# Statistics of all tokens ahead of the first projection, and one bank for both broadcasts, in a two-layer decoder trunk

## The chip, the cores and the metric

The kernel runs on one core of one Trainium2 chip, in one launch. The metric is the device time of that launch in microseconds (us). The kernel before has a median of 1230.92 us over three runs (1229.31, 1230.92 and 1232.93).

Names used throughout: PE is TensorE (matrix products, fp32 results in banks of PSUM), DVE is VectorE, ACT is ScalarE, POOL is GpSimd, SP issues the loads. A "stage" is a stretch of the program, and "k" counts the eight 128-row slices of the 1024 model features.

## The reference

There is one sequence of 512 tokens with 1024 features, two layers, and a conditioning vector c:

```python
def trunk(x, c):                         # cut to what matters
    c_act = silu(c)
    for i in range(2):
        sh1, sc1, g1, sh2, sc2, g2 = split(c_act @ w_mod[i] + b_mod[i], 6)
        h = rms_norm(x, norm_mix[i]) * (1 + sc1) + sh1
        y = stick_breaking_attention(h) if i == 0 else s5_ssm(h)
        x = x + g1 * y
        h = rms_norm(x, norm_ffn[i]) * (1 + sc2) + sh2
        x = x + g2 * conv_ffn(h)         # up-projection, conv of width 3, silu gate, down-projection
    sh, sc = split(c_act @ w_fin + b_fin, 2)
    return rms_norm(x, norm_out) * (1 + sc) + sh
```

`rms_norm` divides each token by the root of the mean square of its 1024 features. So every sub-layer begins with a statistic of each token, which all its 1024 features wait for. The attention's first product is v = h @ w_v, then k and q.

## The kernel before, in words

**Layout.** x stays on the chip, transposed: eight tiles `x[k]` of 128 features by 512 tokens. A product with fp32 accuracy is made of three fast ones (`mm3`, L140 to L146): each operand is split into a high part and a low remainder, and high by high (L142), high by low (L145) and low by high (L146) are summed in a PSUM bank. A weight tile of 128 by 1024 is loaded (`load_w`, L135), ACT writes its high part (L136), and DVE the remainder (L137).

**Normalising.** PE sums the squares over features (`stat`, L234), a matmul of one column for each 128 tokens. ACT takes the root (L238), five small DVE operations invert it (L239 to L243), DVE writes it as diagonals `dg` (L251), and PE broadcasts these over all partitions with a product by ones, which is `rbc` (L256; in the first stage L490). `norm_tile` (L270) then makes one tile of h: DVE multiplies x by rbc into `nt` (L274), ACT applies scale and shift twice (into `hH`, rounded, L284, and into fp32, L285), and DVE subtracts the two to get `hL` (L286).

**Modulation.** The vectors sh, sc and g are matrix-vector products on DVE, one of 128 by 1024 each (`gemv_step`, L167). Those of the first normalisation (16 of them, buffers `wgs`) are made in the first stage, two for each k, ahead of that k's scale and shift.

**First stage** (L471 to L523). The squares are summed on ACT and DVE while x arrives. The statistics run for tokens 0 to 255, and later, behind the first `nt`, for tokens 256 to 511. The two rbc lie in two banks. Tiles k = 0 and 1 are normalised in two halves of 256 tokens, the others whole. Eight banks hold v; each k adds 24 products of 512 columns to them, 192 in all.

**Heads.** The three other sub-layers (feed-forward 0, the state-space layer, feed-forward 1) begin alike: four output banks are filled with tokens 0 to 255 for k = 0 to 7, then with tokens 256 to 511. The statistics of the second half are computed inside the first: at k = 2 its `stat`, and at k = 6 its `rbc` (L256), into a bank of its own. The state-space head computes u, the others `up`.

**What sets the order.** A scheduler puts the instructions of each engine in an order by its own estimate of when their inputs are ready; instructions marked by `keep_in_program_order` (`pe_pin`) keep theirs, and `behind_head` lets some begin only after a given instruction. Each engine then works through its list strictly in order, and waits at an instruction until the semaphores of its inputs have been raised. PE's order in the heads is that of the code: for a k, the four products of hH by the high weights, then the pairs with the low parts.

Of the kernel before, what the change touches and what calls it, by code (L numbers as in the profile page):

```python
# [16 lines left out]
P = 128  # L17
# [50 lines left out]
for _k, _w in _COLS:  # L68
    _OFF[_k] = _n
    _n += _w  # L70
NSMALL = _n

OUT_SHAPE = (2, D * T // 2)
# [7 lines left out]
def _trunk(ctx, tc, I, out, tap):  # L81
# [15 lines left out]
    def bank(p=None, name="ps"):  # L97
        p = p or mm
        return p.tile([P, 512], F32, tag="b", name=name)
# [75 lines left out]
    def mcol(l, v, j):  # L175
        return l * 48 + v * 8 + j
# [77 lines left out]
    def rstd_bc(R, cr, pl, pinned=False):  # L254
        bc = bank(pl, "rbc")
        ins = PE.matmul(bc[:, cr], ones, R["dg"][:, cr], start=True, stop=True)  # L256
        if pinned:
            pe_pin(ins)
        R["bc"][cr.start] = bc
# [9 lines left out]

    def norm_tile(h, k, bc, a, b, cr=FULL, perm=False):  # L270
# [3 lines left out]
        pin["nt"] = V.tensor_tensor(t, x[k][:, cr], bc[:, cr], ALU.mult)  # L274
        first = cr.start == 0 and k == HEADK
        hh, hl = h[0][k][:, cr], h[1][k][:, cr]
        hf = hh.bitcast(F32)
        src = t
        if perm:
            hh, hl = half_cols(h[0][k], cr), half_cols(h[1][k], cr)  # L280
            hf = hh.bitcast(F32)
            u = u.rearrange("p (j c) -> p j c", j=CH)
            src = t.rearrange("p (c j) -> p j c", j=CH)
        act = S.activation(hh, src, AF.Identity, bias=b[:, k:k + 1], scale=a[:, k:k + 1])  # L284
        aff = S.activation(u, src, AF.Identity, bias=b[:, k:k + 1], scale=a[:, k:k + 1])  # L285
        dve = V.tensor_tensor(hl, u, hf, ALU.subtract)  # L286
        if first:
            pin["head"] = [act, aff, dve]
# [80 lines left out]
    def ffn(l, R, prep=None, last=None, hook=lambda: None):  # L369
# [4 lines left out]
        with ExitStack() as fc:  # L374
# [37 lines left out]
            for gi, gn in enumerate((8, 8, 6)):  # L412
# [4 lines left out]
                if gi == 0:  # L417
# [52 lines left out]
    def attention(acc):  # L470
        with ExitStack() as ac:  # L471
            ap = ac.enter_context(tc.tile_pool(name="attn", bufs=1, reuse_waits="tile"))
            wgs = ap.tile([P, 4, D], F32, tag="vn", name="wgs")

            def wmod(col, q):
                SP.dma_start(wgs[:, q, :], I["w_modT"][col * P:(col + 1) * P, :])

            wmod(mcol(0, 1, 0), 0)
            SP.dma_start(consts, I["consts"])
            wmod(mcol(0, 0, 0), 1)  # L480
            SP.dma_start(small, I["small"])
            wv0 = load_w(I["w_v"][0:P, :], name="wv0")
            R = rstd_new(acc)
            R["bc"] = {0: bank(aux, "rbc"), T // 2: bank(mm, "rbc")}
            rb = np_.tile([P, T], F32, tag="sq", bufs=2, name="rb")

            def stat(cr):
                R["ps"] = bank(aux if cr.start == 0 else mm, "stat")
                pin["dg", cr.start] = [rstd_stat(R, cr)]
                PE.matmul(R["bc"][cr.start][:, cr], ones, R["dg"][:, cr], start=True, stop=True)  # L490

            stat(HALF[0])
            h = new_h()
            a = cp.tile([P, KD], F32, tag="Amix0", name="Amix0")
            vb = [bank(mm if i < 6 else aux, f"v{i}") for i in range(8)]
            p0 = None
            for k in range(KD):
                with behind_head(p0) if k in (1, 2) else ExitStack():
                    for v in (1, 0):
                        with behind_head(pin["sum"] if v else pin["dg", 0]):  # L500
                            gemv_step(mcol(0, v, k), False, wgs[:, (2 * k + 1 - v) % 4, :], k > 0)
                    for v in (1, 0):
                        c = mcol(0, v, k)
                        S.activation(mod[:, c:c + 1], raw[:, c:c + 1], AF.Identity, bias=sm("b_mod", c, 1))
                wn = sm("norm_mix", k, 1)
                S.activation(a[:, k:k + 1], mod[:, mcol(0, 1, k):mcol(0, 1, k) + 1], AF.Identity, bias=wn, scale=wn)
                for cr in HALF if k < 2 else (FULL,):
                    if k == 0 and cr.start:
                        with behind_head([pin["nt"]]):
                            stat(cr)  # L510
                        for c in HALF:
                            S.activation(rb[:, c], R["bc"][c.start][:, c], AF.Copy)
                    norm_tile(h, k, R["bc"][cr.start] if k < 2 else rb, a, mod[:, 0:KD], cr)
                    if k == 0:
                        p0 = [pin["nt"]]
                w = wv0
                if k:
                    with behind_head(p0) if k in (1, 2) else ExitStack():
                        w = load_w(I["w_v"][k * P:(k + 1) * P, :], name=f"wv{k}")
                for i in (0, 1, 4, 5, 2, 3, 6, 7):  # L520
                    nb, tt = divmod(i, 4)
                    mm3(vb[i], (h[0][k][:, tt * P:(tt + 1) * P], h[1][k][:, tt * P:(tt + 1) * P]),
                        (w[0][:, nb * 512:(nb + 1) * 512], w[1][:, nb * 512:(nb + 1) * 512]), k == 0, k == KD - 1)  # L523
            last_load = pin["load"]
# [428 lines left out]
    def ssm(R):  # L953
# [3 lines left out]
        with ExitStack() as zc:  # L957
# [4 lines left out]
            for cr in HALF:  # L962
                for k in range(KD):
                    if cr.start == 0 and k == 2:
                        rstd_stat(R, HALF[1], True)
                    if cr.start == 0 and k == 6:
                        rstd_bc(R, HALF[1], mm, True)
                    norm_tile(h, k, R["bc"][cr.start], a, b, cr, perm=True)
                    for w, ps in hd:
# [180 lines left out]
    S.activation(crow, crow, AF.Silu)  # L1150
    sqrt_table()
    pc = [bank(name=f"pc{q}") for q in range(2)]
    for q in range(2):
        PE.matmul(pc[q], ones[0:1, :], crow[:, q * 512:(q + 1) * 512], start=True, stop=True)
    for k in range(KD):
        sq = acc if k == 0 else np_.tile([P, T], F32, tag=("sq", "nt1")[k % 2], bufs=2, name="sq")
        for cr in HALF if k > 6 else (FULL,):
            act = S.activation(sq[:, cr], x[k][:, cr], AF.Square)
            if k:
                add = V.tensor_tensor(acc[:, cr], acc[:, cr], sq[:, cr], ALU.add)  # L1160
                if cr.stop == T // 2:
                    pin["sum"] = [add]
    with behind_head([act]):
        for q in range(2):
            S.activation(cact[:, q * 512:(q + 1) * 512], pc[q], AF.Copy)
    R = attention(acc)
# [163 lines left out]
```

## Time and profile before

| | |
|---|---|
| median of three runs | 1230.92 us |
| the profiled execution | 1231.03 us |
| its span, first to last instruction | 1229.2 us |
| mean granted TensorE clock | 0.987 |
| v stage: first product to last | 19.39 to 69.94 us |
| rbc of the second half in the heads | 292.38 (feed-forward 0), 680.40 (state space), 865.40 us (feed-forward 1) |

A timeline row gives the start, the duration, the engine and line, the operation with its output and inputs, how many alike were joined (x4), and in brackets the idle time before it on its engine with what ended it. Matmuls of a row overlap, so the distance of starts tells the pace better than the duration. A row of windows gives, after the stretch and its length, the busy time and number of instructions on PE, PE's weight loads, DVE, ACT and POOL, then the granted PE clock, the busy share of the DMA engines, and GB/s.

### The profile page before, as it was taken

To read this page: it belongs to the slowest core of one execution; us is meant where nothing else is said; L and a number is where in the kernel's file an instruction comes from. 1 tells how busy PE (TensorE), PEld (TensorE's weight loads), DVE (VectorE), ACT (ScalarE), POOL (GpSimd) and SP (SyncE) were. 2 spreads that over 40 slices of the span, in tenths; PEclk is the share of its full clock that TensorE was granted. 3 is DMA by queue.
4 is the path that set the end of the run, shared out by engine and by line. 5 is a ranking of instruction groups with operands and counts; after the bars stand their busy time and mean duration, and the time that the engine had idled before them with its cause. 6 is when DMAs were issued, how large, how long until landed. Compare 5 with 4: busy or idle time off the path is not lost. (4 is left out here: it accounts for less than half of the span.)

```text
span 1229.2 us, 16696 instructions
## 1 busy us (share of the span) xinstructions
PE 1176.7 (96%) x6244; PEld 967.3 (79%) x6244; DVE 890.1 (72%) x1335; ACT 561.1 (46%) x870; POOL 269.8 (22%) x265
## 2 busy tenths in 40 slices
PE   6999999899999999899998989999999999999997
PEld 4777776589887888678878867689988888888887
DVE  7858888848978778786877559587688458744645
ACT  7646656447543243322345824554843234422434
POOL 1000000000896959876800001000000000000003
PEclk9999999899999999999999989999999999999999
DMA  9764656531438676778555498253256436533211
GB/s 332 282 228 148 204 162 201 157 100 53 138 104 250 218 229 205 217 245 288 164 171 198 161 281 293 89 163 111 84 175 205 129 128 187 160 99 103 81 57 69
DMA packets 93395, 211.02 MB, mean 172 GB/s; under 512 B 19585, under 2 KB 39681, under 8 KB 93314
## 3 DMA queue, kind: packets, MB, share of 16 engines
q1 hardware_dynamic: 93314, 209.96, 53.4%
q8 instruction: 49, 0.80, 0.3%
q14 instruction: 32, 0.26, 0.1%
HBM read 188.68 MB, written 21.24 MB: 171 GB/s over the span
## 5 line engine op out<-in xcount | busy, mean ns | idle before, releaser
L145 PE MATMUL up<-hL,up_h 128*128 128x512 f32 (+1 forms) x704 | 265.8, 380 | 0.0
L146 PE MATMUL up<-hH,up_l 128*128 128x512 f32 (+1 forms) x704 | 265.6, 379 | 0.0
L142 PE MATMUL up<-hH,up_h 128*128 128x512 f32 (+1 forms) x704 | 262.2, 381 | 0.0
L137 DVE TENSOR_TENSOR up_l<-up_r,up_h 128x1024 fp32r<-128x1024 f32 x84 | 119.7, 1426 | 58.4 <-ACT up_h L136 57.3
L136 ACT ACTIVATE up_h<-up_r 128x1024 fp32r<-128x1024 f32 x84 | 88.4, 1056 | 156.5 <-PE dn L145 74.5
L142 PE MATMUL dn<-gH,dn_h 128*128 128x512 f32 (+1 forms) x394 | 146.7, 374 | 6.9 <-ACT gH L397 6.6
L146 PEld LDWEIGHTS up<-hH,up_l 128*128 128x128 f32 x704 | 132.4, 188 | 25.1
L145 PEld LDWEIGHTS up<-hL,up_h 128*128 128x128 f32 x704 | 132.4, 188 | 24.5
L142 PEld LDWEIGHTS up<-hH,up_h 128*128 128x128 f32 x704 | 129.9, 188 | 26.1 <-issue 0.8
L145 PE MATMUL dn<-gL,dn_h 128*128 128x512 f32 (+1 forms) x394 | 146.4, 371 | 0.7 <-DVE gL L398 0.5
L146 PE MATMUL dn<-gH,dn_l 128*128 128x512 f32 (+1 forms) x394 | 145.8, 370 | 0.0
L167 DVE SCALAR_TENSOR_TENSOR wg<-wg,cact 128x1024 f32<-128x1024 f32 x96 | 128.4, 1352 | 23.6 <-DMA wg<-in_w_modT_dram 23.2
L1202 POOL TENSOR_SCALAR xa<-x,Anorm_out 128x256 f32<-128x256 f32 x7 | 5.9, 847 | 445.1 <-DVE x L303 445.0
L142 PEld LDWEIGHTS dn<-gH,dn_h 128*128 128x128 f32 x394 | 75.3, 191 | 21.1 <-ACT gH L397 8.3
L137 DVE TENSOR_TENSOR dn_l<-dn_r,dn_h 128x1024 fp32r<-128x1024 f32 (+1 forms) x48 | 63.5, 1332 | 34.7 <-ACT dn_h L136 34.4
L145 PEld LDWEIGHTS dn<-gL,dn_h 128*128 128x128 f32 x394 | 75.5, 192 | 14.3 <-DVE gL L398 2.0
L146 PEld LDWEIGHTS dn<-gH,dn_l 128*128 128x128 f32 x394 | 75.5, 192 | 12.2
L303 DVE SCALAR_TENSOR_TENSOR x<-dn,mod,x 128x512 f32<-128x512 f32 (+1 forms) x55 | 37.1, 679 | 64.1 <-PE dn L146 64.1
L397 ACT ACTIVATE gH<-gm 128x512 fp32r<-128x512 f32 x44 | 27.8, 631 | 119.3 <-DVE gm L394 119.3
L136 ACT ACTIVATE dn_h<-dn_r 128x1024 fp32r<-128x1024 f32 (+1 forms) x48 | 46.6, 982 | 63.3 <-PE dn L145 37.6
L387 DVE SCALAR_TENSOR_TENSOR ca<-up,small,ca 128x511 f32<-128x511 f32 x88 | 65.1, 741 | 5.6 <-ACT ca L386 5.6
L386 ACT ACTIVATE ca<-up,small 128x512 f32<-128x512 f32 x88 | 66.7, 761 | 5.3 <-PE up L146 5.3
(300 smaller groups left out, 2359.0 us busy)
## 6 DMA issues: line engine op xcount, KB each, us to landing
wg<-in_w_modT_dram SPq DMA_DIRECT2D x96, 512.0 KB
up_r<-in_w_up_dram SPq DMA_DIRECT2D x84, 512.0 KB
dn_r<-in_w_down_dram SPq DMA_DIRECT2D x32, 512.0 KB
wgs<-in_w_modT_dram SPq DMA_DIRECT2D x16, 512.0 KB
dn_r<-in_w_down_dram SPq DMA_DIRECT2D x16, 384.0 KB
wv_r<-in_w_v_dram SPq DMA_DIRECT2D x8, 512.0 KB
wk_r<-in_w_qk_dram SPq DMA_DIRECT2D x8, 512.0 KB
wq_r<-in_w_qk_dram SPq DMA_DIRECT2D x8, 512.0 KB
```

The source lines that it names most:

```text
L136: S.activation(wh[:, :n], raw[:, :n], AF.Copy)
L137: V.tensor_tensor(wl[:, :n], raw[:, :n], wh[:, :n].bitcast(F32), ALU.subtract)
L142: ins = PE.matmul(ps, ah, bh, start=start, stop=False)
L145: PE.matmul(ps, ah, bl, start=False, stop=False)
L146: PE.matmul(ps, al, bh, start=False, stop=stop)
L167: ins = V.scalar_tensor_tensor(w, w, 1.0, cact, ALU.mult, ALU.mult, accum_out=raw[:, col:col + 1])
L303: V.scalar_tensor_tensor(xs, pv, gate, xs, ALU.mult, ALU.add)
L386: S.activation(ca, ps, AF.Identity, bias=small[:, cb:cb + 1], scale=tapw[2])
L387: V.scalar_tensor_tensor(ca[:, 1:], ps[:, :T - 1], tapw[1], ca[:, 1:], ALU.mult, ALU.add)
L397: S.activation(gh, m, AF.Copy)
L1202: G.tensor_scalar(xa[k], x[k][:, cb], a[:, k:k + 1], 0.0, ALU.mult, ALU.add)
```

## The change

It has four parts.

1. **First stage, statistics.** The eight adds of squares are whole (the last was in halves). Four `stat` columns, one root and one set of small operations serve all 512 tokens. Four diagonals are written, and both rbc follow at once, into one bank, ahead of every normalised tile. ACT's load of the table of roots moves from before the squares to behind the first half of `cact`; the second half of `cact` is copied on DVE instead of ACT.
2. **First stage, weights and tiles.** The first w_v tile is split by halves of 512 columns (ACT and DVE); only k = 0 is normalised in halves. From k = 1 on DVE's order is fixed: modulation product for shift of k, remainder of w_v(k), modulation product for scale of k+1, hL(k), nt(k+1). ACT's and SP's instructions of this loop are fixed too; loads are issued two tiles ahead.
3. **small.** The table of biases and norms is loaded in two parts (168 columns, the rest later).
4. **Heads.** `rstd_bc` puts the second half's rbc into the bank of the first half, if there is one. This holds in all three heads, whose `norm_tile` reads `R["bc"][0]` for both halves.

```diff
     def rstd_bc(R, cr, pl, pinned=False):
-        bc = bank(pl, "rbc")
+        bc = R["bc"].get(0) or bank(pl, "rbc")
         ins = PE.matmul(bc[:, cr], ones, R["dg"][:, cr], start=True, stop=True)
...
                             if cr.start == 0 and k == 6:
-                                rstd_bc(R, HALF[1], mm, True)
-                            norm_tile(h, k, R["bc"][cr.start], a, b, cr)
+                                rstd_bc(R, HALF[1], None, True)
+                            norm_tile(h, k, R["bc"][0], a, b, cr)
...
-            stat(HALF[0])
-            h = new_h()
-            for k in range(KD):
...
-                for cr in HALF if k < 2 else (FULL,):
-                    if k == 0 and cr.start:
-                        with behind_head([pin["nt"]]):
-                            stat(cr)
...
+            gv(1, 0)
+            y = rstd_y(R, FULL, True)
+
+            def spread(cr):
+                for i in range(cr.start // P, cr.stop // P):
+                    V.tensor_scalar(R["dg"][:, i * P:(i + 1) * P], ident, y[:, i:i + 1], None, ALU.mult)
+                rstd_bc(R, cr, None, True)
+
+            spread(HALF[0])
+            spread(HALF[1])
+            gv(0, 0)
...
+            for q, cr in enumerate(HALF):
+                norm_tile(h, 0, R["bc"][0], a, mod[:, 0:KD], cr, pinned=True, mid=lambda: low0(q))
+            pe_pin(S.activation(rb, R["bc"][0], AF.Copy))
+            prods(0, wv0)
+            w = high(1)
+            gv(1, 1)
+            for k in range(1, KD):
+                def mid():
+                    nxt[0] = high(k + 1) if k < KD - 1 else None
+                    pe_pin(V.tensor_tensor(w[1], raws[k], w[0].bitcast(F32), ALU.subtract))
+                    if k < KD - 1:
+                        gv(1, k + 1)
+
+                nxt = [None]
+
+                def first():
+                    gv(0, k)
+                    if k + 2 < KD:
+                        raws[k + 2] = loads(k + 2)
+
+                norm_tile(h, k, rb, a, mod[:, 0:KD], FULL, False, True, first, mid)
+                prods(k, w)
+                w = nxt[0]
```

What this does to the engines' lists is seen at two places. The first is DVE in the v stage. In these rows x_78 is x[0], x_79 is x[1] and so on; the first `nt` of x_80 belongs to k = 2. Before:

```order
L137 TENSOR_TENSOR wv_l<-wv_r,wv_h 128x1024 [waits DMAHW0_49,Activation_49]
L286 TENSOR_TENSOR hL_195<-nt_242,hH_187 128x256 [waits Activation_49]
L274 TENSOR_TENSOR nt_284<-x_79,rbc 128x256 [waits DVE_49]
L167 SCALAR_TENSOR_TENSOR wgs,modraw<-wgs,cact 128x1024 [waits DMAHW2_49]
L137 TENSOR_TENSOR wv_l<-wv_r,wv_h 128x1024 [waits DMAHW1_49,Activation_49]
L167 SCALAR_TENSOR_TENSOR wgs,modraw<-wgs,cact 128x1024 [waits DMAHW3_49]
L286 TENSOR_TENSOR hL_196<-nt_279,hH_188 128x256 [waits Activation_49]
L274 TENSOR_TENSOR nt_327<-x_80,rb 128x512 [waits DVE_49]
```

And after the change, from the first normalised tile:

```order
L275 TENSOR_TENSOR nt_226<-x_78,rbc 128x256 [waits PE_49]
L554 TENSOR_TENSOR wv_l<-wv_r,wv_h 128x512 [waits DMAHW5_49,Activation_49]
L297 TENSOR_TENSOR hL_201<-nt_227,hH_193 128x256 [waits Activation_49]
L275 TENSOR_TENSOR nt_234<-x_78,rbc 128x256
L554 TENSOR_TENSOR wv_l<-wv_r,wv_h 128x512 [waits Activation_49]
L297 TENSOR_TENSOR hL_201<-nt_235,hH_193 128x256 [waits Activation_49]
L168 SCALAR_TENSOR_TENSOR wgs,modraw<-wgs,cact 128x1024 [waits DMAHW6_49]
L275 TENSOR_TENSOR nt_272<-x_79,rb 128x512 [waits DVE_49,Activation_49]
L168 SCALAR_TENSOR_TENSOR wgs,modraw<-wgs,cact 128x1024 [waits DMAHW7_49]
L574 TENSOR_TENSOR wv_l<-wv_r,wv_h 128x1024 [waits DMAHW0_49,Activation_49]
L168 SCALAR_TENSOR_TENSOR wgs,modraw<-wgs,cact 128x1024 [waits DMAHW2_49]
L297 TENSOR_TENSOR hL_202<-nt_273,hH_194 128x512 [waits Activation_49]
```

Before, the weights' remainders and modulation products of later k stood ahead of an hL; after it, each k has its two `wgs`, one `wv_l`, one hL and one nt, in a fixed turn. The numbers of lines are one to some sixty higher.

The second place is DVE in the head of the state-space layer, around k = 6 of the first half (x_84 is x[6], x_85 is x[7]; x_78 begins the second half). Before:

```order
L274 TENSOR_TENSOR nt_6218<-x_84,rbc 128x256
L243 SCALAR_TENSOR_TENSOR ny<-ntm,ny 128x2 [waits DVE_49]
L251 TENSOR_SCALAR dg<-consts,ny 128x128 [waits DVE_49]
L286 TENSOR_TENSOR hL_6076<-nt_6199,hH_6068 128x8x32 [waits Activation_49]
L274 TENSOR_TENSOR nt_6236<-x_85,rbc 128x256
L137 TENSOR_TENSOR win_l<-win_r,win_h 128x1024 [waits DMAHW7_49,Activation_49]
L137 TENSOR_TENSOR win_l<-win_r,win_h 128x1024 [waits DMAHW0_49,Activation_49]
L137 TENSOR_TENSOR win_l<-win_r,win_h 128x1024 [waits DMAHW3_49,Activation_49]
L286 TENSOR_TENSOR hL_6077<-nt_6219,hH_6069 128x8x32 [waits Activation_49]
L274 TENSOR_TENSOR nt_6254<-x_78,rbc 128x256 [waits PE_49]
```

And after the change:

```order
L252 TENSOR_SCALAR dg<-consts,ny 128x128 [waits DVE_49]
L297 TENSOR_TENSOR hL_6056<-nt_6179,hH_6048 128x8x32 [waits Activation_49]
L138 TENSOR_TENSOR win_l<-win_r,win_h 128x1024 [waits DMAHW0_49,Activation_49]
L138 TENSOR_TENSOR win_l<-win_r,win_h 128x1024 [waits DMAHW1_49,Activation_49]
L138 TENSOR_TENSOR win_l<-win_r,win_h 128x1024 [waits DMAHW4_49,Activation_49]
L275 TENSOR_TENSOR nt_6197<-x_84,rbc 128x256 [waits PE_49]
L275 TENSOR_TENSOR nt_6215<-x_85,rbc 128x256
L297 TENSOR_TENSOR hL_6057<-nt_6198,hH_6049 128x8x32 [waits Activation_49]
L275 TENSOR_TENSOR nt_6233<-x_78,rbc 128x256 [waits DVE_49]
```

The multiplication for k = 6 of the first half has moved behind the three `win_l`, and it, not the first one of the second half, now waits for PE. The value it waits for is that of the second half's rbc, which PE's list holds, before and after, between the products of k = 5 and those of k = 6:

```order
L147 MATMUL u_6073<-hH_6048,win_l 128x8x32
L257 MATMUL rbc<-dg,ones 128x256
L143 MATMUL u_6070<-hH_6049,win_h 128x8x32 [waits Activation_49]
L143 MATMUL u_6071<-hH_6049,win_h 128x8x32
L143 MATMUL u_6072<-hH_6049,win_h 128x8x32
L143 MATMUL u_6073<-hH_6049,win_h 128x8x32
L146 MATMUL u_6070<-hL_6057,win_h 128x8x32 [waits DVE_49]
```

The heads of the two feed-forwards have the same new wait at the same k. There is one difference more: the scheduler deals out a few dozen instructions of attention and of the feed-forwards, and the state-space preparation on POOL, in a somewhat other order.

More of the change, by code (lines that the diff above doesn't have):

```diff
@@ L274, in norm_tile @@
         pin["nt"] = V.tensor_tensor(t, x[k][:, cr], bc[:, cr], ALU.mult)
-        first = cr.start == 0 and k == HEADK
+        head = cr.start == 0 and k == HEADK
         hh, hl = h[0][k][:, cr], h[1][k][:, cr]
@@ L482, in attention @@
[L482 to L490, printed above, removed]
-            stat(HALF[0])
@@ new lines, in attention @@
+            high0(0)
+            h = new_h()
+            vo = (0, 1, 4, 5, 2, 3, 6, 7)
+            vb = [None] * 8
+            for n, i in enumerate(vo):
+                vb[i] = bank(mm if n < 6 else aux, f"v{i}")
+            raws = {1: loads(1)}
+            SP.dma_start(small[:, NMOD:], I["small"][:, NMOD:])
+            raws[2] = loads(2)
+            for q, cr in enumerate(HALF):
+                norm_tile(h, 0, R["bc"][0], a, mod[:, 0:KD], cr, pinned=True, mid=lambda: low0(q))
+            pe_pin(S.activation(rb, R["bc"][0], AF.Copy))
@@ L1156, in _trunk @@
         sq = acc if k == 0 else np_.tile([P, T], F32, tag=("sq", "nt1")[k % 2], bufs=2, name="sq")
[L1157 to L1165, printed above, removed]
+        act = S.activation(sq, x[k], AF.Square)
+        if k:
+            add = V.tensor_tensor(acc, acc, sq, ALU.add)
+    with behind_head([act, add]):
+        S.activation(cact[:, 0:512], pc[0], AF.Copy)
+        V.tensor_copy(cact[:, 512:], pc[1])
+        sqrt_table()
     R = attention(acc)
```

90 lines of the change are left out of this document (59 added, 31 removed).

## The prediction

> **What bounds the kernel now.** I read the page first, then PE's waits, then windows over the stretches that the change touches, then timelines. The page, by engine:
>
> ```profile
> span 1229.2 us, 16696 instructions
> PE 1176.7 (96%) x6244; PEld 967.3 (79%) x6244; DVE 890.1 (72%) x1335; ACT 561.1 (46%) x870; POOL 269.8 (22%) x265
> ```
>
> PE is busy for 96% of the span. A change pays here only through PE's remaining idle time (1229.2 − 1176.7 = 52.5 us) or through the clock at which it works. PE's waits that this change can reach:
>
> ```profile
> PE v L146 <- DVE hL L286: 3.0, 2, 2.7
> PE u L142 <- ACT hH L284: 1.5, 1, 1.5
> ```
>
> The columns are us in total, times, longest. The v stage loses 3.0 us to a late hL, and one head has 1.5 us for an hH. The stretches (busy time of PE, its loads, DVE, ACT, POOL, then clock, DMA share, GB/s):
>
> ```profile
> 19.40:36.40 17.00, 16.73 (x66) 13.04 (x64) 16.00 (x27) 13.80 (x25) 0.00 (x0) 1.00 0.97 345
> 36.40:39.20 2.80, 0.05 (x2) 0.00 (x1) 2.80 (x5) 1.17 (x5) 0.00 (x0) 1.00 1.02 339
> 39.20:43.40 4.20, 4.20 (x11) 3.34 (x12) 4.20 (x7) 2.44 (x3) 0.00 (x0) 0.59 0.93 366
> 43.40:69.90 26.50, 26.50 (x118) 21.96 (x117) 17.18 (x24) 14.28 (x25) 0.00 (x0) 1.00 0.56 194
> ```
>
> PE is idle from 36.4 to 39.2 while DVE is busy throughout, and in the next 4.2 us its clock is 0.59 of full. So the late hL costs twice: the idle time, and a slow spell behind it. From 43.4 on PE has no gap, and DVE works 17.18 of 26.50 us: DVE was late at one place only, by its order. The timeline of PE:
>
> ```profile
> 11.72 1.87 PE L234 MATMUL stat<-ones,acc 128*128 128x1 f32 x8 [4.65 <-DVE acc L1160]
> 14.66 1.22 PE L490 MATMUL rbc<-dg,ones 128*128 128x256 f32 x2 [1.07 <-DVE dg L251]
> 19.39 0.99 PE L142 MATMUL v<-wv_h,hH 128*128 128x512 f32 x1
> 20.17 0.63 PE L145 MATMUL v<-wv_l,hH 128*128 128x512 f32 x1
> 20.60 0.63 PE L142 MATMUL v<-wv_h,hH 128*128 128x512 f32 x1
> ...
> 39.20 3.22 PE L146 MATMUL v<-wv_h,hL 128*128 128x512 f32 x8 [2.75 <-DVE hL L286]
> ...
> 69.71 0.39 PE L146 MATMUL v<-wv_h,hL 128*128 128x512 f32 x1
> 69.94 0.39 PE L142 MATMUL k<-hH,wk_h 128*128 128x512 f32 x1
> ```
>
> At full clock the pitch of these products is 69.94 − 69.71 = 0.23, or 26.50 / 118 = 0.2246 by the last window; I take the middle, 0.2275. The 192 products of v then need 43.7 us, and took 69.94 − 19.39 = 50.55. Of the 6.9 between, 3.0 are the two waits for hL; the eleven products from 39.2 to 43.4 took 4.2 instead of 2.5, so 1.7 is the slow spell behind the long wait; the rest, 2.2, is the start of v, where the pitch is 20.60 − 20.17 = 0.43.
>
> **The change, first stage.** When can v begin? DVE's rows for it:
>
> ```profile
> 8.06 3.94 DVE L1160 TENSOR_TENSOR acc<-acc,sq 128x512 f32<-128x512 f32 x6 [0.22 <-ACT sq L1158]
> 13.28 0.15 DVE L239 TENSOR_SCALAR nv<-stat 128x2 f32<-128x2 f32 x1
> 14.12 0.48 DVE L251 TENSOR_SCALAR dg<-consts,ny 128x128 f32<-128x128 f32 x2
> 15.92 0.42 DVE L274 TENSOR_TENSOR nt<-x,rbc 128x256 f32<-128x256 f32 x1 [0.17 <-PE rbc L490]
> ...
> 36.17 1.22 DVE L137 TENSOR_TENSOR wv_l<-wv_r,wv_h 128x1024 fp32r<-128x1024 f32 x1
> 37.31 1.22 DVE L167 SCALAR_TENSOR_TENSOR wgs<-wgs,cact 128x1024 f32<-128x1024 f32 x1
> 38.45 0.69 DVE L286 TENSOR_TENSOR hL<-nt,hH 128x512 fp32r<-128x512 f32 x1
> 39.06 0.69 DVE L274 TENSOR_TENSOR nt<-x,rb 128x512 f32<-128x512 f32 x1
> ```
>
> The adds end at 12.0. The four columns of stat take 1.87 (13.87); root and hand-overs bring the small operations to 14.2; they take 14.12 − 13.28 = 0.84 (15.05); the first two diagonals 0.48, when the first rbc begins. The two rbc take about a microsecond each, so both are there at 17.7, and nt of half 0, which now waits for both, follows at once. From nt to hH is 0.45 and hH takes 0.60 (rows of this size, at 293.01 and 293.46 below), so v begins near 18.8, 0.6 earlier than at 19.39. The half copy of cact and the modulation product that now stand ahead of `nv` on DVE (0.7 and 1.2, by the rows of their sizes at 38.45 and 37.31) fit between 12.0 and 14.2, beside stat and the root. The load of the table of roots, now on ACT between cact and the root, lies there too; a table load takes 1.28 here:
>
> ```profile
> 3.26 1.28 ACT L224 ACT_TABLE_LOAD   x1
> ```
>
> Without its cover it would cost that much at most, which the range takes in. Afterwards each k costs DVE two modulation products, one remainder (1.14 each by the starts 36.17, 37.31, 38.45), one hL and one nt (0.61 each, by 38.45 and 39.06): 4.64 us. PE needs 24 × 0.2275 = 5.46 per k. PE begins k = 1 at about 18.8 + 5.5 + 2.2 = 26.5, and its list takes hL(1) behind sixteen products, at 30.1; DVE's rows in the new order, laid end to end from nt at 17.7, end hL(1) near 27.4. The margin then grows by 0.8 per k. So both waits for hL go (3.0), and with the long one the slow spell behind it (1.7). The next thing to be late would be a load: 1.57 MB per k (two wgs and one w_v of 0.52 MB) at the 345 GB/s of the first window is 4.6 us, below 5.46 but not far. The slow spell at v's start remains.
>
> Sum: 3.0 + 1.7 + 0.6 = **5.3 us gained**. Lower bound 3.6 (the spell at the start lasts twice as long, −1.7), upper 6.1 (it is half as long). From 69.94 on PE works on k without a gap, so I carry all of it to the end; the reordered rows of attention I price at nothing, ±1.5, from PE's small gaps there.
>
> **The change, heads.** The list of the changed DVE has one new wait: nt of k = 6, half 0, waits until the second half's rbc is done on PE. PE's list has nothing between that rbc and the products of k = 6. So PE must stand while nt(6), then hH(6), are made. Before, nt(6) and hH(6) were made ahead. The state-space head now:
>
> ```profile
> 679.81 3.49 DVE L137 TENSOR_TENSOR win_l<-win_r,win_h 128x1024 fp32r<-128x1024 f32 x3 [0.19 <-ACT win_h L136]
> 680.40 0.60 PE L256 MATMUL rbc<-dg,ones 128*128 128x256 f32 x2
> 681.57 0.84 ACT L284 ACTIVATE hH<-nt,mod,Anorm_mix 128x256 fp32r<-128x256 f32 x1
> 682.31 0.85 ACT L285 ACTIVATE nt<-nt,mod,Anorm_mix 128x256 f32<-128x256 f32 x1
> 682.46 0.74 PE L142 MATMUL u<-hH,win_h 128*128 128x256 f32 x4 [1.46 <-ACT hH L284]
> 683.22 0.41 DVE L286 TENSOR_TENSOR hL<-nt,hH 128x256 fp32r<-128x256 f32 x1
> 683.69 0.39 PE L145 MATMUL u<-hL,win_h 128*128 128x256 f32 x1 [0.49 <-DVE hL L286]
> ```
>
> In the new list nt(6) stands behind the three win_l, so it begins at 683.22. The hand-over from nt to hH is 0.45 (293.46 − 293.01 below): hH at 683.67. From hH to PE is 682.46 − 681.57 = 0.89: 684.56, so PE stands about 3.6 us instead of 1.46. The second ACT pass starts 0.74 behind hH and takes 0.85; hL begins at about 685.33 and PE follows 683.69 − 683.22 = 0.47 later, at 685.80 instead of 683.69: **+2.1**. The two feed-forward heads:
>
> ```profile
> 293.01 0.42 DVE L274 TENSOR_TENSOR nt<-x,rbc 128x256 f32<-128x256 f32 x1 [0.60 <-PE rbc L256]
> 293.28 0.28 PE L145 MATMUL up<-hL,up_h 128*128 128x256 f32 x1
> 293.46 0.60 ACT L284 ACTIVATE hH<-nt,mod,Anorm_ffn 128x256 fp32r<-128x256 f32 x1 [0.77 <-DVE nt L274]
> 293.97 0.59 ACT L285 ACTIVATE nt<-nt,mod,Anorm_ffn 128x256 f32<-128x256 f32 x1
> ...
> 866.53 0.41 DVE L286 TENSOR_TENSOR hL<-nt,hH 128x256 fp32r<-128x256 f32 x1
> 867.00 0.39 PE L145 MATMUL up<-hL,uph_h 128*128 128x256 f32 x1 [0.54 <-DVE hL L286]
> ```
>
> In feed-forward 0 DVE is free, and the row at 293.01 shows when an nt that waits for this rbc can begin. Then hH at 293.46, the second pass at 293.97 to 294.56, hL, and PE at 295.07 instead of 293.28: **+1.8**. In feed-forward 1 nt(6) takes the place at 866.53, behind weight remainders; hH 866.98, second pass 867.48 to 868.07, PE at 868.6 instead of 867.00: **+1.6**. Behind nt(6) on DVE are queued nt(7), hL(6) and the second half's tiles; they only shift with it. The sum of the heads is 5.5 us. From below: if the weight remainders come after nt(6) or earlier than now, the two later heads fall to some 1.0 each, 3.8 in all; from above 6.5, with 0.3 more at each for the hand-overs. The price of a rbc without this wait is nothing, as before.
>
> Here the Trainium skill speaks against the shared bank: its page "PSUM — Partial Sum Buffer", section "PSUM bank collisions raise a hardware error", says that two engines on one bank and quadrant of partitions collide even at disjoint columns, so that accesses must be ordered by bank, not by address. With such an order the sum has the 5.5 us of the heads; by addresses alone nt(6) would be free, and the time would be that of the first rival below.
>
> Last, the clock. An idle time of 2.75 us was followed by a window at 0.59; the state-space head's 1.46 and 0.49 were not:
>
> ```profile
> 682.50:690.00 7.50, 6.95 (x50) 6.36 (x51) 4.50 (x11) 7.50 (x11) 0.00 (x0) 1.00 0.92 338
> ```
>
> Its new 3.6 us exceed the 2.75, so I expect a slow spell there, 1.7 us as at 39.20, less the 0.55 that PE has free in the window behind it, where ACT with 7.50 of 7.50 sets the pace: **+1.2**; bounds 0 (no spell) and 1.7.
>
> The Trainium skill, page "TensorE: Matmul & The Clock Gate", section "Part 1: The HAM clock gate", tells of a free-running window of about 3.4 us and half clock after one idle window. Taken strictly, 2.75 us could not have done it, and 3.6 us would only rarely; an estimate by that page is 1231.2 in place of my sum. The trace's 0.59 behind 2.75 us decides for the spell.
>
> **Sum.** The profiled execution took 1231.03 us (span 1229.2 and 1.8 around it), 0.11 above the median of the runs. 1231.03 − 5.3 + 5.5 + 1.2 = 1232.4; less 0.1 for the median, 1232.3. What is given back in the heads cancels what the v stage gains.
>
> **Rivals.**
>
> *The heads cost nothing* (0.22). The first stage gains its 5.3, and the new wait is met before it matters, or the delay is taken up later by slack in the heads. For it: the three heads are followed by PE's weight of work, but also by waits for ACT (the 7.50 of 7.50). Against it: the list has rbc directly ahead of k = 6 with no other PE work. Time: 1231.0 − 5.3 = 1225.7.
>
> *The clock falls in all three heads* (0.18), slower than before. Place: PE's idle time between rbc and hH(6) is about 1.2 us in feed-forward 0 and 1.6 in feed-forward 1, with some 0.3 to 0.5 more before hL. It decides from the point where the idle share in one stretch of some 3.4 us (the length of a slow spell here) is over about half; 1.46 + 0.49 in the old state-space head was not enough. Price: 1.7 us each, in full at the state-space head. Time: 1231.0 − 5.3 + 5.5 + 3 × 1.7 = 1236.3.
>
> *The change doesn't do what it says* (0.08): the loads can't keep the fixed turn. For it: the DMA share is 0.97 and 1.02 up to 39.2. Against it: 4.6 us against 5.46 per k. PE would then wait for wv_h instead of hL, the slow spell stays, and the gain is 1 at most: 1231.0 − 1 + 5.5 + 1.2 = 1236.7.
>
> **How the numbers follow.** The forecast has 0.52, with its own range 1229 to 1235.5 from the terms' bounds. About 0.3% (3.7 us) is what a measurement of this kernel can tell from no change: faster is below 1227.2, slower above 1234.6. Of the forecast 0.01 lies below, 0.41 between, 0.10 above; of the first rival 0.18 below and 0.04 between; of the second 0.05 between and 0.13 above; of the third 0.02 between and 0.06 above. Rounded: faster 0.19, same 0.52, slower 0.29. The range 1225.2 to 1237.3 leaves out about 0.1 at each end.
>
> **What would show it.** *v stage:* PE without a wait for hL between 20 and 64 us, clock 1.00 from the fifth microsecond of v, the first product of k near 64.6; a wait for wv_h would prove the third rival. *Heads:* PE idle between rbc and hH(6) in all three, with nt as the chain's origin and starting directly behind rbc or the weight remainders; no such idle time proves the first rival. *Clock:* a window near 0.6 behind the state-space head alone; behind all three, the second rival. The forecast would be wrong above all if the 5.3 us were lost later in attention, or if the scheduler's other order there cost or saved more than 1.5 us.

## The result, and the profile after

The changed kernel has a median of 1237.9 us over five runs (1235.44 to 1242.19), the kernel before 1230.92. The ratio is 1.0059, with a 95% interval of 1.0043 to 1.0075: 0.4 to 0.75% slower, some 7 us. Forecast was 1232.3 us, no measurable change, in a range up to 1237.3. The profiled execution took 1235.44 us, the quickest of the five, so its trace shows 4.4 of the 7 us.

The page of the changed kernel, and then PE's waits in it (us in total, times, longest):

```profile
span 1233.6 us, 16690 instructions
PE 1177.2 (95%) x6244; PEld 967.6 (78%) x6244; DVE 885.6 (72%) x1329; ACT 561.2 (45%) x865; POOL 270.7 (22%) x265
```

```profile
PE dn L143 <- ACT gH L410: 7.9, 3, 4.2
...
PE u L143 <- ACT hH L289: 3.8, 2, 3.6
PE t L687 <- DVE om L675: 3.5, 4, 1.6
PE z L669 <- DVE q_nt L649: 3.3, 2, 2.0
...
PE up L143 <- ACT hH L289: 2.8, 2, 1.6
```

PE works as long as before (1177.2 against 1176.7 us); what was added is waiting. The wait for a late hL in v is gone from the list. These five waits were smaller or absent before; against them, attention's wait for q_sq fell from 2.0 to 0.2 us. (gH is the high part of the gated activations that the down-projection, `dn`, multiplies; om, q_nt and q_sq are tiles of attention that DVE makes and PE reads.) The same rows before:

```profile
PE dn L142 <- ACT gH L397: 6.6, 3, 4.4
...
PE t L623 <- DVE om L611: 1.7, 3, 0.8
PE z L605 <- DVE q_nt L585: 1.6, 2, 0.9
PE u L142 <- ACT hH L284: 1.5, 1, 1.5
```

Following the same matmul through both traces shows where the time went. In the v stage the changed kernel moves ahead: the first k product stands at 65.09 us instead of 69.94, so 4.8 us ahead. At 212 us it is still 4.8 ahead, at 235 only 2.9. Behind the head of feed-forward 0 it is 1.0 ahead; after that feed-forward's first group of down-projections 2.2 behind. From there to 670 us it comes back to 1.2 ahead, since slow spells behind waits that both kernels have (near 523 and 663 us) were shorter or absent in this execution. Behind the state-space head it is 2.8 behind, and from feed-forward 1 to the end 4.3.

**The v stage** in windows, the same stretches as before (the last ends where v ends):

```profile
36.40:39.20 2.80, 2.80 (x14) 2.33 (x13) 2.80 (x5) 1.81 (x5) 0.00 (x0) 1.00 1.00 367
39.20:43.40 4.20, 4.20 (x20) 3.46 (x20) 4.20 (x8) 3.05 (x6) 0.00 (x0) 1.00 0.98 349
43.40:65.10 21.70, 21.70 (x98) 17.96 (x97) 17.78 (x23) 15.00 (x23) 0.00 (x0) 1.00 0.87 282
```

PE is busy throughout at a clock of 1.00, and does 20 products from 39.2 to 43.4 where it did 11. The loads kept up.

**The heads** have the new idle time. These rows of PE's timeline are the first products of k = 6 in feed-forward 0, the state-space layer and feed-forward 1, and in the feed-forwards where the next hL joins (in brackets the idle time before them):

```profile
291.25 0.74 PE L143 MATMUL up<-hH,up_h 128*128 128x256 f32 x4 [1.15 <-ACT hH L289]
292.20 0.38 PE L146 MATMUL up<-hL,up_h 128*128 128x256 f32 x1 [0.22 <-DVE hL L297]
...
683.41 1.22 PE L143 MATMUL u<-hH,win_h 128*128 128x256 f32 x4 [3.56 <-ACT hH L289]
...
870.37 0.74 PE L143 MATMUL up<-hH,uph_h 128*128 128x256 f32 x4 [1.63 <-ACT hH L289]
871.32 0.38 PE L146 MATMUL up<-hL,uph_h 128*128 128x256 f32 x1 [0.21 <-DVE hL L297]
```

Measured along the trace up to that hL they cost 1.9, 2.1 and 1.6 us. The four products at 683.41 take 1.22 instead of 0.74: the clock is at half, and with this slow spell the state-space head costs 3.9.

**A wait that nobody had on the list** is the one for gH in feed-forward 0. ACT's, PE's and SP's timelines there, after the change:

```profile
374.83 1.06 ACT L137 ACTIVATE dn_h<-dn_r 128x1024 fp32r<-128x1024 f32 x1 [8.29 <-DMA dn_r<-in_w_down_dram]
```

```profile
384.42 0.73 PE L143 MATMUL dn<-gH,dn_h 128*128 128x512 f32 x2 [2.73 <-ACT gH L410]
```

```profile
346.00 2.28 SPq L136 DMA_DIRECT2D dn_r<-in_w_down_dram  x3
369.64 0.38 SPq L904 DMA_DIRECT2D sR<-tb  x1
370.11 0.46 SPq L136 DMA_DIRECT2D dn_r<-in_w_down_dram  x1
```

And SP before:

```profile
344.27 15.73 SPq L135 DMA_DIRECT2D dn_r<-in_w_down_dram  x4
371.16 0.38 SPq L840 DMA_DIRECT2D sR<-tb  x1
```

Before, four weight loads of the down-projection were issued ahead of `sR<-tb`, a transfer of the state-space preparation that waits for POOL. After, only three were; the fourth load stood behind that transfer until 369.64. ACT waited 8.29 us for this load, everything behind it in ACT's order was late, gH among it, and PE waited 2.73 us at 384.42 instead of 1.08. A spell of 3.4 us at half clock followed.

### The profile page after: what moved, and what is told of

Same layout as the page of the kernel before. It is cut to its first block, busy times and chain, and to the rows that moved or that the text cites. A ratio compares the mean times of both kernels' runs of the same rounds, so it can differ in the third digit from the quotient of the medians.

```text
span 1233.6 us, 16690 instructions
## 1 busy us (share of the span) xinstructions
PE 1177.2 (95%) x6244; PEld 967.6 (78%) x6244; DVE 885.6 (72%) x1329; ACT 561.2 (45%) x865; POOL 270.7 (22%) x265
## 5 line engine op out<-in xcount | busy, mean ns | idle before, releaser
L138 DVE TENSOR_TENSOR up_l<-up_r,up_h 128x1024 fp32r<-128x1024 f32 x84 | 125.4, 1495 | 56.0 <-ACT up_h L137 55.1
```

Of the source, the lines that this page charges most:

```text
L138: V.tensor_tensor(wl[:, :n], raw[:, :n], wh[:, :n].bitcast(F32), ALU.subtract)
```

## The experiments

Ratios are to the kernel before, timed on the same chip, with the 95% interval; the last column is what the ratio differs from 1, times 1231, in us. The runs were timed on several chips, so between two runs this column says more than the medians.

| run | median, us | ratio | against before |
|---|---|---|---|
| the change | 1237.9 | 1.0059 (1.0043 to 1.0075) | +7.3 |
| own banks in the heads | 1229.83 | 0.9994 (0.9983 to 1.0005) | −0.7 |
| heads only | 1242.02 | 1.0097 (1.0078 to 1.0117) | +11.9 |
| tiles first | 1230.09 | 0.9993 (0.9981 to 1.0005) | −0.9 |
| late attention | 1228.86 | 0.9981 (0.9969 to 0.9993) | −2.3 |
| load order | 1233.41 | 1.0020 (1.0009 to 1.0031) | +2.5 |
| state head only | 1231.94 | 1.0006 (0.9995 to 1.0018) | +0.7 |
| state head filled | 1229.57 | 0.9987 (0.9974 to 1.0000) | −1.6 |
| filled | 1225.59 | 0.9952 (0.9938 to 0.9965) | −5.9 |

**Own banks in the heads: the first stage alone.** The change, with the heads undone:

```diff
-        bc = R["bc"].get(0) or bank(pl, "rbc")
+        bc = (R["bc"].get(0) if pl is None else None) or bank(pl, "rbc")
...
-    rstd_bc(R, HALF[1], None, True)
-    norm_tile(h, k, R["bc"][0], a, b, cr)
+    rstd_bc(R, HALF[1], mm, True)
+    norm_tile(h, k, R["bc"][cr.start], a, b, cr)
```

> The changed kernel, but in the three heads the second half's rbc has its own bank again, as before; the first stage stays changed. Theory (the two halves of the change are independent; the first stage gains, the heads and what follows from them lose): v ends 4.8 us earlier, no idle time of PE ahead of hH(6) in the feed-forward heads, 1.5 us in the state-space head, the wait dn <- gH near 384 us back at 1.1 us from 2.7, and 1226 to 1228 us, clearly faster than before. Rival (the first stage's gain is lost later in attention, where the changed profile shows 1.9 us given back between 212 and 228 us, or in the load queue): 1230 to 1233 us, no faster than before, with the wait dn <- gH still at 2.7.

Measured: 1229.83 us, the interval of the ratio holding 1: no measurable gain. The v stage is 4.7 us ahead, and the wait for gH near 381 us is back at 1.1, as the theory has it; the time is the rival's. So the heads and the load queue are the loss, and the first stage's gain doesn't arrive either. Its profiled execution is 5.0 us ahead at 212, 2.8 at 235 and 2.4 at the end.

**Heads only: the kernel before with the shared bank.**

```diff
-        bc = bank(pl, "rbc")
+        bc = R["bc"].get(0) or bank(pl, "rbc")
...
-    rstd_bc(R, HALF[1], mm, True)
-    norm_tile(h, k, R["bc"][cr.start], a, b, cr)
+    rstd_bc(R, HALF[1], None, True)
+    norm_tile(h, k, R["bc"][0], a, b, cr)
```

> The kernel before, with only the second half's rbc put into the first half's bank in the three heads. Theory (the heads cost their waits, and the freed bank lets the scheduler put a transfer that waits for POOL ahead of a weight load in feed-forward 0): 5.6 us in the heads, 1.6 us in the wait dn <- gH, up to 3.4 us of slower clock behind them: 1238 to 1242 us. Rival (only the waits of the heads cost; the late load came from the first stage's other timing): 1236 to 1237 us, with dn <- gH at 1.1 us.

Measured: 1242.02 us, 11 to 12 above the kernel before, at the upper edge of the theory. The wait for gH at 386 us is 2.57 us, so the shared bank, in this order, makes the load late without the first stage's change: the scheduler gives SP's list another order. These are SP's rows in the kernel before, and then in this one:

```
L135 DMA dn_0_2_r<-in_w_down_dram 128x1024 [waits DMAHW4_49,DVE_49]
L135 DMA dn_0_3_r<-in_w_down_dram 128x1024 [waits DMAHW6_49,DVE_49]
L840 DMA sR<-tb 128x4x256 [waits Pool_49]
```

```
L135 DMA dn_0_2_r<-in_w_down_dram 128x1024 [waits DMAHW4_49,DVE_49]
L840 DMA sR<-tb 128x4x256 [waits Pool_49]
L135 DMA dn_0_3_r<-in_w_down_dram 128x1024 [waits DMAHW6_49,DVE_49]
```

The fourth load, dn_0_3, has changed places with the transfer that waits for POOL. The changed kernel's list has the same exchange.

The loss is more than the other runs leave for it: the change less own banks, which holds the same heads and the same exchange, is 8.0 us. So the parts don't add up. The first stage's change is worth 0.7 us with own banks and 4.6 with the shared one (the change less heads only), 3.9 apart with some 3.4 to either side; no run shows why.

This run shows one thing more. Its v stage is that of the kernel before, with the same wait, yet the clock behind it differs:

```profile
35.90:38.90 3.00, 0.25 (x3) 0.01 (x1) 3.00 (x7) 1.71 (x5) 0.00 (x0) 1.00 1.04 365
38.90:43.10 4.20, 4.20 (x18) 3.48 (x19) 4.20 (x7) 3.33 (x6) 0.00 (x0) 1.00 1.00 399
```

18 products at a clock of 1.00, where the kernel before had 11 at 0.59. The slow spell behind this wait isn't certain.

**Tiles first: the same bank, other order.** The change, with the last two tiles of the first half written ahead of the rbc:

```diff
-    if cr.start == 0 and k == 6:
-        rstd_bc(R, HALF[1], None, True)
-    norm_tile(h, k, R["bc"][0], a, b, cr)
+    if cr.start or k < 7:
+        norm_tile(h, k, R["bc"][0], a, b, cr)
+    if cr.start == 0 and k == 6:
+        norm_tile(h, 7, R["bc"][0], a, b, cr)
+        rstd_bc(R, HALF[1], None, True)
```

> The changed kernel with its shared bank, but in each head the normalised tiles k = 6 and 7 of the first half are written ahead of the second half's rbc, so that they need not wait for it; PE's order is the same. Theory (the price is the order within the bank, not the bank): heads as before, 1226 to 1228 us, the same as with a bank of its own within 0.2%. Rival (sharing a bank costs by itself, since rbc must now wait for DVE's reads, or reads and writes slow each other): 1231 us or more, with PE waiting for nt ahead of rbc in the heads.

Measured: 1230.09 us, with own banks 1229.83. The theory's equality holds, with some 2 us to either side (its absolute figure was too low, like that of the own-bank run). One bank costs nothing that can be told if every read of the first half is written ahead of the second half's write. The price was the wait that the order made.

The run also says what moved the weight load. The bank is shared here too, yet SP issues four loads ahead of the transfer again:

```profile
342.19 15.72 SPq L136 DMA_DIRECT2D dn_r<-in_w_down_dram  x4
369.07 0.38 SPq L906 DMA_DIRECT2D sR<-tb  x1
```

So the freed bank doesn't exchange them, as the expectation of heads only had it. Where the list is left to the scheduler, the exchange stands only in the runs whose feed-forward 0 has the new wait in its head (the change, heads only). That the scheduler counts this wait in its own estimate of readiness, and so puts the load later, is concluded and not shown.

**Late attention.** The run with own banks, with one subtraction moved to POOL:

```diff
-        V.tensor_tensor(wl[:, :n], raw[:, :n], wh[:, :n].bitcast(F32), ALU.subtract)
+        (low or V).tensor_tensor(wl[:, :n], raw[:, :n], wh[:, :n].bitcast(F32), ALU.subtract)
...
-    load_w(wsrc(mt), name=f"wo{mt}")
+    load_w(wsrc(mt), name=f"wo{mt}", low=G if mt == 2 else None)
```

The reason lies in DVE's timeline of the own-bank run, and PE's beside it:

```profile
213.57 1.22 DVE L675 TENSOR_TENSOR_SCAN om<-om,maskb 128x512 f32<-128x512 f32 x1
214.70 1.20 DVE L138 TENSOR_TENSOR wo_l<-wo_r,wo_h 128x1024 fp32r<-128x1024 f32 x1
215.82 1.21 DVE L675 TENSOR_TENSOR_SCAN om<-om,maskb 128x512 f32<-128x512 f32 x1
```

```profile
217.09 0.69 PE L687 MATMUL t<-consts,om 128*128 128x128 f32 x2 [1.81 <-DVE om L675]
220.63 0.58 PE L669 MATMUL z<-kB,q_nt 128*128 128x256 f32 x1 [2.03 <-DVE q_nt L649]
```

A weight remainder stands between two scans that PE waits for; before the change the scans stood together, and the longest of PE's waits here were 0.8 us for om and 1.2 for q_sq.

> The run with its own bank, with one edit in late attention: the low part of the third output-projection weight (the subtraction that stood between the last two om scans) is made on POOL instead of DVE, and the om scans stand together again, as in the kernel before. Theory (the first stage's gain is given back in late attention, where the scheduler put that subtraction, 1.2 us, ahead of an om scan that PE waits for, and the longer idle time lengthens the spell at half clock from 6.8 to 10.2 us): PE's waits for om and q_nt between 213 and 221 us fall from 5.5 to at most 4.5 us, the spell is 6.8 us, and the time is 1.5 to 3 us below that of the own-bank run, 1227 to 1228.5. Rival (the 2.2 us given back come from elsewhere, for instance the clock's phase alone): the time stays within 0.7 us of 1229.8.

Measured: 1228.86 us, 1.0 below the own-bank run by the medians and 1.6 by the ratios, with intervals that overlap: this doesn't decide between the theory's 1.5 and the rival's 0.7. The waits for om, q_sq and q_nt from 213 to 222 us fell from 5.5 to 4.2 us and the spell to 6.8 us, which is seen in the window from 210 to 230 us, of the own-bank run and of this one in turn:

```profile
210.00:230.00 20.00, 14.19 (x60) 9.62 (x59) 16.57 (x26) 8.44 (x18) 0.00 (x0) 0.74 0.42 133
```

```profile
210.00:230.00 20.00, 15.69 (x68) 10.44 (x67) 18.31 (x29) 10.09 (x21) 0.00 (x0) 0.83 0.51 154
```

A clock of 0.74 over 20 us is 10.4 us at half, 0.83 is 6.8, as before the change. But a new wait for om of 1.44 us stands at 195.68, and the edit also takes 1.2 us of work from DVE. In this execution a spell of 3.4 us at half clock stood at 84 us too, and took it from 5.8 us ahead of the kernel before to 3.4. That the subtraction's place lengthens the spell is shown; that this explains all the time given back in late attention is not.

**Load order.** The changed kernel, with the two transfers put behind the weight loads again (`pin` holds the load's instruction):

```diff
     for ri in range(2):
-        SP.dma_start(sR[hb * 4:(hb + 1) * 4, :, ri, :].rearrange("b p n -> p b n"), tb[:, ri].rearrange("p (b q) c -> p b (q c)", b=4))
+        with (behind_head([pin[f"lddn0_0_{3 + ri}"]]) if hb and f"lddn0_0_{3 + ri}" in pin else ExitStack()):
+            SP.dma_start(sR[hb * 4:(hb + 1) * 4, :, ri, :].rearrange("b p n -> p b n"), tb[:, ri].rearrange("p (b q) c -> p b (q c)", b=4))
```

> The changed kernel, shared bank and all, but the third and fourth transfer of the state-space preparation that wait for POOL (sR <- tb) are issued behind the weight loads dn 3 and dn 4 of feed-forward 0, as they were in the kernel before. Theory (1.65 us of idle time, and often a slow spell behind it, come from dn 3 standing behind a transfer that waits for POOL): the wait dn <- gH near 384 us goes from 2.7 to 1.1 us, ACT no longer waits 8 us for a dn_r load, and the time is 1.6 to 3.3 us below 1237.9: 1234.5 to 1236.5. Rival (the load would be as late anyway, since the head's delay shifts everything): the wait stays above 2.3 us and the time within 0.7 us of the changed kernel's.

Measured: 1233.41 us, 4.5 below the change, more than the theory's 3.3. The wait at 384 us isn't 1.1 us but gone from the trace altogether. PE comes there 0.9 us later than in the kernel before, because of feed-forward 0's head, and ACT starts this gH at 381.85 us instead of 383.07. Behind it PE is 0.8 ahead, so of the heads' 5.6 us 1.7 are taken up there: the run does more than put the list back.

**State head only, and filled.** The own-bank run with the shared bank in the state-space head alone; then the same with products on PE that nothing reads, between rbc and k = 6:

```diff
+    fill = bank(mm, "fill")
+    for _ in range(26):
+        pe_pin(PE.matmul(half_cols(fill, HALF[0]), hd[0][0][0][:, 0:P], half_cols(h[0][5], HALF[0]), start=True, stop=True))
```

> The own-bank run, with the shared bank in the state-space head alone. Theory (2.1 us of waiting and up to 3.4 us of slower clock): idle time of PE ahead of hH(6) is 3.6 us instead of 1.5, and the time is 2.1 to 4.5 us above the own-bank run's 1229.8: 1232 to 1234.3. Rival (the head's delay is taken up later, the loss lies in the feed-forward heads): at most 1 us above, under 1231.

> As the run with the shared bank in the state-space head alone, with 26 products of 256 columns put on PE between the rbc and the products of k = 6, into a spare bank that nothing reads: PE is busy for about 3.1 us of the 3.6 us that it waits. Theory (part of the head's price is the clock, which falls behind PE's idle time): no spell at half clock behind this head, and 1.5 to 2.5 us below the run without the filling, 1230.5 to 1232. Rival (the clock behind this head doesn't depend on the idle time, or the waits alone make the price): within 0.7 us of the run without the filling, or slower, with a spell at half clock all the same.

Measured: 1231.94 without the filling, 2.1 above the own-bank run by the medians (the theory's lower edge; 1.3 by the ratios, inside the noise), and 1229.57 with it, 2.4 below. The windows show why, first without (rbc, idle time and the spell), then with it:

```profile
678.40:681.90 3.50, 0.02 (x1) 0.02 (x1) 2.88 (x4) 1.50 (x3) 0.00 (x0) 0.89 0.74 208
681.90:688.70 6.80, 6.80 (x31) 6.33 (x32) 3.06 (x9) 6.80 (x10) 0.00 (x0) 0.56 0.90 328
```

```profile
678.40:681.90 3.50, 3.50 (x29) 3.38 (x27) 3.37 (x5) 1.50 (x3) 0.00 (x0) 1.00 0.50 156
681.90:688.70 6.80, 5.89 (x43) 5.24 (x42) 3.03 (x8) 6.80 (x10) 0.00 (x0) 1.00 0.95 334
```

The products of k = 6 start at 681.88 and 682.39, later if anything. But in the next 6.8 us PE does 31 products at 0.56 in the one and 43 at 1.00 in the other. The wait and the clock are two prices, and the second fell away when these 26 products filled the wait.

**Filled: a version that beats both.** The late-attention run with 11 such products in the state-space head, and 17 of 512 columns in feed-forward 0's longest wait (this edit alone is shown):

```diff
+            if mt == 0 and nm == "dn0_1_":
+                fill = bank(aux, "fill")
+                for _ in range(17):
+                    pe_pin(PE.matmul(fill, w[0][:, 0:P], rhs[0][0], start=True, stop=True))
             run(ps, w, FULL, k0=k0, pinned=mt < len(part))
```

> The late-attention run (first stage changed, own banks, one subtraction on POOL) with two fillings of PE that nothing reads: 11 products of 256 columns between rbc and k = 6 in the state-space head, where PE waits 1.5 us, and 17 products of 512 columns (3.9 us) ahead of the last products of the second down-projection group in feed-forward 0, where PE waits 4.3 us. Theory (the clock falls behind PE's idle time, and filling this time keeps it): no spell at half clock near 521 and 680 us, and 1.5 to 4 us below the late-attention run's 1228.9: 1225 to 1227.4, faster than both kernels. Rival (the spells follow a window's phase whatever PE does there, or the filling delays what comes after): within 0.7 us of 1228.9 or slower.

Measured: 1225.59 us, ratio 0.9952 (0.9938 to 0.9965), faster than both kernels, and 3.6 us below late attention by the ratios, as the theory has it. Behind the filled wait the window has full clock, here the kernel before and then this run:

```profile
521.20:528.00 6.80, 4.73 (x21) 3.37 (x25) 3.77 (x5) 2.60 (x3) 0.26 (x1) 0.50 0.98 287
```

```profile
519.80:527.00 7.20, 6.97 (x42) 5.21 (x43) 6.38 (x9) 2.17 (x3) 4.19 (x3) 1.00 1.03 324
```

**The kernel before, once more.**

> The kernel before, profiled once more. Theory (the window that sets the clock runs free, so the same wait of 2.75 us in the v stage brings a slow spell in some executions and not in others): the idle time near 36 to 39 us is again 2.7 to 2.8 us, and spells at half clock stand behind other waits than in the first profile. Rival (the spell belongs to the wait): again a clock near 0.6 from 39.2 to 43.4 us, and spells at the same six places.

Measured: 1231.39 us. The wait was 2.73 us at 38.72, and the slow spell stood behind it again:

```profile
39.20:43.40 4.20, 4.20 (x14) 3.24 (x13) 4.20 (x8) 2.91 (x7) 0.00 (x0) 0.61 1.01 400
```

The other spells stood at the same places too, one of them of another length. This is what the rival expected, but the run can't decide between the two, as the traces show. In all of them the stretches at one clock, from the first at full clock to the last change, are whole multiples of 3.413 us (in the kernel before 17.07, 3.41, 177.49 and 6.83 us: 5, 1, 52 and 2 of them), so the clock is set by windows of this length that follow each other without a gap. These are the windows that hold most of the wait, in the kernel before, in this run and in heads only:

```profile
36.48:39.89 3.41, 0.69 (x3) 0.61 (x4) 3.41 (x6) 1.78 (x5) 0.00 (x0) 1.00 0.94 317
36.68:40.09 3.41, 1.37 (x6) 1.15 (x7) 3.41 (x6) 1.97 (x4) 0.00 (x0) 1.00 1.01 363
37.21:40.63 3.42, 1.73 (x8) 1.44 (x9) 3.42 (x6) 1.94 (x4) 0.00 (x0) 1.00 0.98 361
```

PE is busy for 0.69, 1.37 and 1.73 us of them, and the clock of the next window is 0.50, 0.50 and 1.00. The same holds over all eleven traces, without their first and last few windows: of the windows at full clock, all 49 in which PE was busy for under 45% were followed by one at half, none of the 3680 with over 55% was, and 7 of the 20 between. So the same wait brings a spell or none by where it falls in the windows; the windows of this execution lay within 0.2 us of those of the first.

## Why the prediction was wrong, step by step

By the runs, the 7.3 us are made of: first stage −0.7 (own banks), heads +3.2 (load order less own banks), load queue +4.8 (the change less load order). The ratios have 1.4 to 2 us to either side, their differences about 2 for the heads and 2.4 for the queue. The parts depend on the runs that they are taken from: heads only, which holds heads and queue, costs 11.9 where these two sum to 8.0. The forecast was −5.3, +5.5 + 1.2, and nothing.

- **"When can v begin"** was right but for 0.3 us: 19.11 instead of 18.8. stat began 0.2 later than taken, and rbc 0.3.
- **"Both waits for hL go, and with the long one the slow spell"**: right in the trace. 4.8 us were gained at the end of v against 5.3. The 1.7 us of the spell were taken as certain, though; the heads-only run had the wait without it. So over many executions the v stage may gain less than the one profile shows.
- **"I carry all of it to the end; the reordered rows of attention I price at nothing, ±1.5"** is the first step that failed. Between 212 and 235 us 1.9 to 2.2 us are given back in the change and in the own-bank run, by longer waits for om and q_nt and a spell of 10 us instead of 7. In some executions a second spell stands near 84 us, behind two waits of 1.1 and 1.3 us for q_sq and q_nt that were 0.8 and 0.7 before. This is the window of the load-order run there:

```profile
84.50:88.00 3.50, 3.50 (x11) 2.81 (x11) 2.87 (x6) 3.44 (x8) 0.00 (x0) 0.53 0.42 129
```

  The clock is 0.53. Together this leaves, with own banks, a gain that can't be told from none. DVE is busy for 19.2 of 20 us in late attention before the change: the working goes by the windows of v, and has none of the stage that had to carry the gain.
- **The heads, "+1.8, +2.1, +1.6"**: measured along the trace 1.9, 2.1, 1.6. The working of this part, from the new wait in the list to the end of each chain, held in every step. That the sum came out at 3.2 in the medians has one reason that shows, the 1.7 us that the load-order run takes up at gH; that the clock's price differs between executions may be another.
- **"Last, the clock: +1.2"**: the mechanism held (filling the idle time took the spell away), the size was low. Filling was worth 2.4 us. Behind the wait of 3.6 us the spell lasted two windows of 3.4 us in two traces (the change, state head only) and one in two others (heads only, load order); the forecast counted one.
- **What was left out** is the largest part. "There is one difference more" was known of the list, and I priced it only in attention. With the shared bank in this order, a weight load on SP's queue changed places with a transfer that waits for POOL. The load-order run puts 4.8 us on this; along the trace the change lost 3.2 there, and the other 1.7 are what that run gains at the same gH over the kernel before. The exchange was to be read from SP's list before the run, and its price from the row at 371.16: a transfer that couldn't start before that time, with a load now behind it.

Of the rivals, *the clock falls in all three heads* gave 1236.3, near the median, but that nearness is luck: in the profiled execution no spell followed the two feed-forward heads. Its condition, an idle share of over about half in a stretch of 3.4 us, is what the windows bear out. PE was busy for 2.13 and 1.78 of 3.41 us in the windows of these heads (from 290.18 and 867.03), enough to keep the clock; in the heads-only run it was 1.56 (from 870.07), and a spell stood behind feed-forward 1. "The heads cost nothing" falls by the traces. "The change doesn't do what it says" falls too: the loads kept pace.

What stays open: how much of the time given back in late attention is the order of DVE's list, how much is that this stretch is bound by DVE anyway, and why the first stage is worth more beside the shared bank than without it.

## What to carry to other kernels

A wait that a change brings into one place can change a scheduler's order elsewhere: compare the lists of every engine, the load queue first, and look for a load that has moved behind something that waits for another engine. Where a buffer is shared between two halves, write all reads of the first ahead of the write of the second; then sharing cost nothing here that could be told. And a gain early in a program is worth what the stages behind it let through, so read their windows before carrying the gain to the end.

## What the runs showed of the hardware

PE's clock falls by windows of 3.41 us behind idle time, and what decided here was PE's busy share in the window before: under 45% always brought half clock, over 55% never. So the same wait brings no slow window, one or two in different executions: none or one behind 2.75 us in v, none in the kernel before but one in the own-bank run behind 1.46 us in the state-space head, one or two behind 3.56 us there. Products whose result nobody reads keep the clock up: 17 of them, 3.9 us in a wait of 4.3, left a window at 1.00 where it was 0.50. With 11 more in the state-space head and the edit in late attention this is the quickest version here.
